# Scores of two differential heads in one run, with the work around the runs in a written order

## The chip, the cores and the metric

The kernel runs on one core of a Trainium2 chip. The metric is the time of one execution on the device in microseconds (us); the time given for a kernel is the median of its runs. The engines are TensorE (PE, matmuls; its weight loads are listed as PEld), VectorE (DVE), ScalarE (ACT), GpSimd (POOL) and SyncE (SP, which issues the loads of weights).

## The reference

A two-layer encoder over 256 tokens of 2048 features, in float32. One layer, with the parts that the change does not touch in a line each:

```python
h = rmsnorm(x, g_mix[i])
dq, dk, dv, cq, ckv, kr, ga, gb = split(h @ w_in[i])
# differential attention: 8 heads, two softmax maps of 64 features each
dq, dk = apply_partial_rope(dq), apply_partial_rope(dk)
scores = einsum('bqhcd,bkhcd->bhcqk', q, k) * 64 ** -0.5
probs = softmax(scores)
weights = probs[:, :, 0] - lam * probs[:, :, 1]
od = einsum('bhqk,bkhe->bqhe', weights, dv)
od = rmsnorm(od, g_subln[i]) * (1 - lam_init)
# latent attention: 8 heads, q and k from low-rank latents, one shared rotary key
om = latent_attention(q_nope, q_rope, k_nope, k_rope, v_mla)
m = sigmoid(ga) * (od @ w_branch_diff[i]) + sigmoid(gb) * (om @ w_branch_mla[i])
x = x + m @ w_out[i]
x = x + swiglu(rmsnorm(x)) ; x = x + sigmoid(rmsnorm(x) @ w_ple_gate[i]) * (p[i] @ w_ple_in[i])
```

## The kernel before, in words

**Precision.** Activations and weights are kept as two parts in TensorE's fast float32 format, a high part and a low part (the rest). A product of a 128-column block of weights with activations is made of pairs of matmuls (`emit`): one of the high weights with both parts of the activations, 512 columns (line 226), and one of the low weights with the high part, 256 columns (line 230). A product over 2048 features has 16 such pairs and one PSUM bank of 512 float32 as its accumulator.

**Weights.** `piece` loads up to eight 128x128 blocks by SP's queue into a buffer `w32` (line 198), ScalarE makes the high part `whi` (line 201) and VectorE the low part `wlo` (a subtraction by the helper at line 78). There are four buffers for loads and three for high parts, so the preparation runs ahead of TensorE by as many pieces.

**Products leave PSUM** in `joined`: ScalarE copies one half (line 256), VectorE adds the other. `split` makes the two parts of a result.

**The differential stage** of a layer goes through these functions. `queries_keys(h)` makes query and key of head h: two products, each joined, rotated with a shuffle (line 577) and three more operations of VectorE, and split. `scores` multiplies them in three terms (high by low, low by high, high by high) for two blocks of 128 queries. The two maps of a head have 64 features each, so their matmuls use 64 rows of the array, one map the upper and one the lower half; they are issued in turns, twelve to a head (line 428). `exps` is the softmax: maximum on VectorE (line 434), exponential and sum on ScalarE (line 437), reciprocal on VectorE (line 438). `diff_weights` joins the two maps (ScalarE line 691, VectorE line 81). `turned` transposes the weights by four matmuls with the identity (line 446) and `diff_out` multiplies them with the values in eight matmuls (line 701). `settle` normalizes four heads and transposes them (line 716).

**Order.** `pipelined` traces the scores of head h+1 ahead of the transposes of head h, and takes steps of the generator `beside` in between: keys of the latent heads (`keys_up`), queries and keys of the next differential head, the shared rotary key (`narrow`, line 414, and `rotated`, line 380), gates and latent queries. What is traced is not yet the order on the engines. A scheduler takes each engine's instructions in the order in which a simulated run has them ready, those traced earlier first; `keep_in_program_order` ties an instruction behind the one traced before it on the same engine, for the order of issue only. After the differential stage come the latent heads (`mla_weights`, `mla_out`, scores also at line 428, in full height), the two branches, the output product, the feed-forward part and the last gate.

**PSUM.** The eight banks are three pools: four banks `mm` for products, two `S` for scores, two `at` for the rest.

Of the kernel before, what the change touches and what calls it, by code (L numbers as in the profile page):

```python
# [56 lines left out]
def encoder(ctx, tc, x, p, positions, cols, lams, wq, wk, wv, wcq, wckv, wkr, wga, wgb,  # L57
# [9 lines left out]
    ps_mm = pool("ps_mm", 4, space=PSUM)  # L67
    ps_s = pool("ps_s", 2, space=PSUM)
# [5 lines left out]
    def bank(ps=ps_at, tag="at", name="at", shape=(P, 2 * T)):  # L74
        return ps.tile(list(shape), F32, tag=tag, name=name)
# [344 lines left out]
    def scores(*maps):  # L420


        Ss = [bank(ps_s, "S", "S", (P, 2, T)) for _ in maps]
        for b in range(2):
            for j in range(len(maps[0])):
                for S, pairs in reversed(list(zip(Ss, maps))):
                    q, k = pairs[j]
                    PE.matmul(S[:, b, :], q[:, b * P : (b + 1) * P], k, start=j == 0, stop=j == len(pairs) - 1)  # L428
        return Ss
# [97 lines left out]
    for L in range(DEPTH):  # L527
# [72 lines left out]
        def keys_up(n):  # L600
            for acc in pair(w_kn[L, n : n + 2], ckv):
                kn.append(operand(fb(len(kn), F32R)))
                split(kn[-1], joined(acc))
# [22 lines left out]
        def beside():  # L626

            for h in range(2, DH):
                if h < 6:
                    keys_up(2 * h - 4)  # L630
                elif h == 7:
                    rotated(joined(narrow(wkr[L], ua)), crm, srm)
                yield
                queries_keys(h)
                yield
            for n in (8, 0, 2, 10):
                if n == 0:
                    settle(0)
                gate(wga, gate_a, next(todo))
                queries_up(n)  # L640
                yield
            settle(4)
            for n in (4, 6):
                gate(wga, gate_a, next(todo))
                queries_up(n)
            gate(wga, gate_a, next(todo))

# [32 lines left out]
        fill = beside()  # L680
# [3 lines left out]
        def diff_weights(h):  # L684
            q, k = qk[h]
            E = [weights(), weights("E1")]
            halves = [slice(c * 64, (c + 1) * 64) for c in range(2)]
            r = [exps(S, e, 0.125) for S, e in zip(scores(*(three(q[d], k[d]) for d in halves)), E)]
            ts(r[1], r[1], neg_lam[:, L : L + 1], None, ALU.mult)
            for b in range(2):  # L690
                A.activation(E[0][:, b, :], E[0][:, b, :], AF.Copy, scale=r[0][:, b : b + 1])
                stt(E[0][:, b, :], E[1][:, b, :], r[1][:, b : b + 1], E[0][:, b, :], ALU.mult, ALU.add)
            return E[0]
# [36 lines left out]
        pipelined(diff_weights, diff_out, DH, lambda: next(fill, None))  # L730
        for _ in fill:
            pass
# [4 lines left out]
        def mla_weights(h):  # L737
            E = weights()
            t = slice(h % 2 * T, (h % 2 + 1) * T)
            S, = scores(three(qn[h], kn[h]) + [(qr[h // 2][:, t], krs[1][:, t]), (qr[h // 2][:, t], krs[0][:, :T])])  # L740
            r = exps(S, E, MLA_SCALE)
            for b in range(2):
                ts(E[:, b, :], E[:, b, :], r[:, b : b + 1], None, ALU.mult)
            return E
# [179 lines left out]
    def S_bank():  # L924
        return operand(bank(ps_s, "S", "S", (P, 2, T)))

    def mm_bank():
        return bank(ps_mm, "mm", "mm")

# [12 lines left out]
    t0 = [transposed(0, q, get()) for q, get in enumerate((S_bank, S_bank, mm_bank, mm_bank))]  # L942
# [13 lines left out]
    t1.append(transposed(1, 3, S_bank()))  # L956
# [92 lines left out]
```

## Time and profile before

| what | value |
|---|---|
| time, median of 3 runs (lowest to highest) | 2825.21 us (2825.15 to 2825.63) |
| the profiled execution | 2825.27 us |
| its span in the trace | 2823.5 us |
| granted clock of TensorE | 0.999 |
| PE busy | 2815.7 us, 16691 matmuls |
| DVE busy | 2080.0 us |
| ACT busy | 1532.0 us |
| matmuls at line 428 of 64 rows | 192 |

A row of the timeline gives the start of an instruction (or of several of one kind) in us, its length, engine, line, operation, output and inputs with their shapes, and the count. Matmuls are pipelined: one starts long before the one ahead has ended, so what a matmul costs TensorE is the time from its start to the next start, and the lengths overlap. A row of the chain gives start, length, engine and line. A row of the groups gives after the bar the busy time in us and the mean of one in ns, and after the second bar the engine's idle time ahead of them. A row of the waits says who waited for whom, for how many us in total, how often, and the longest.

### The profile page before, as it was taken

The numbers are of one execution on the slowest core, as the hardware profiler recorded it, in microseconds if no ns is written. First come the engines' busy times: TensorE is split into PE (matmuls) and PEld (weight loads), VectorE is DVE, ScalarE is ACT, GpSimd is POOL, SyncE is SP. The second block draws the span as 40 slices with busy tenths as digits, with TensorE's granted clock in tenths as the row PEclk, the third lists the DMA queues.
The fourth block names the chain that finished last, engine by engine and source line by source line (L and its number), as shares of the span: only waits on it lengthen the run. The fifth ranks groups of instructions, "written<-read, shape, count | busy, mean of one in ns | idle before, by whom it ended". The sixth has DMA issues, their size and how long they took to land.

```text
span 2823.5 us, 43989 instructions
## 1 busy us (share of the span) xinstructions
PE 2815.7 (100%) x16691; PEld 2489.4 (88%) x16691; DVE 2080.0 (74%) x3566; ACT 1532.0 (54%) x2554; POOL 3.1 (0%) x17
## 2 busy tenths in 40 slices
PE   9999999999999999999999999999999999999999
PEld 8888988888888888888888889888888888888888
DVE  8898668776666666677869976687766666666777
ACT  7676546554444444455646765465544444444556
POOL 0000000000000000000000000000000000000000
PEclk9999999999999999999999999999999999999999
DMA  7545455555665566566554454555556655655654
GB/s 247 174 162 172 157 187 198 194 193 194 186 200 193 188 195 197 193 193 193 194 193 166 157 172 158 194 198 193 194 193 189 199 193 185 202 194 194 193 193 157
DMA packets 158180, 531.36 MB, mean 188 GB/s; under 512 B 17168, under 2 KB 25360, under 8 KB 157968
## 3 DMA queue, kind: packets, MB, share of 16 engines
q1 hardware_dynamic: 157536, 527.96, 56.8%
q8 instruction: 131, 2.15, 0.3%
q10 hardware_dynamic: 432, 0.59, 0.1%
q14 instruction: 81, 0.66, 0.1%
HBM read 526.39 MB, written 2.10 MB: 187 GB/s over the span
## 4 chain that ended last, share of the span: by engine, by line
PE 100%; DMA 0%; DVE 0%; ACT 0%; DVEq 0%; issue 0%
PE mm L226 61%; PE mm L230 31%; PE S L428 1%; PE mmv L501 1%; PE mmv L502 1%; PE mmv L503 1%; PE at L446 1%; PE at L701 1%; PE mm L848 0%; PE at L757 0%; PE mm L414 0%; PE at L716 0%; PE mmv L472 0%; DMA gcol<-in_cols 0%; PE at L339 0%; PE at L307 0%
## 5 line engine op out<-in xcount | busy, mean ns | idle before, releaser
L201 ACT ACTIVATE whi<-w 128x1024 fp32r<-128x1024 f32 (+2 forms) x1038 | 1064.3, 1026 | 1225.6 <-issue 592.8
L78 DVE TENSOR_TENSOR wlo<-w,whi 128x1024 fp32r<-128x1024 f32 (+2 forms) x1038 | 1225.7, 1181 | 645.7 <-ACT whi L201 635.1
L226 PE MATMUL mm<-ub,whi 128*128 128x512 f32 x3936 | 1340.5, 389 | 0.0
L226 PE MATMUL mm<-ua,whi 128*128 128x512 f32 x3712 | 1274.8, 390 | 0.0
L230 PE MATMUL mm<-ub,wlo 128*128 128x256 f32 x3936 | 1084.6, 276 | 0.0
L230 PE MATMUL mm<-ua,wlo 128*128 128x256 f32 x3712 | 1027.8, 277 | 0.0
L226 PEld LDWEIGHTS mm<-ub,whi 128*128 128x128 f32 x3936 | 737.7, 188 | 152.4
L226 PEld LDWEIGHTS mm<-ua,whi 128*128 128x128 f32 x3712 | 696.2, 188 | 141.2
L230 PEld LDWEIGHTS mm<-ub,wlo 128*128 128x128 f32 x3936 | 738.8, 188 | 1.3
L230 PEld LDWEIGHTS mm<-ua,wlo 128*128 128x128 f32 x3712 | 697.0, 188 | 1.9
L78 DVE TENSOR_TENSOR a<-mm,join 128x256 f32<-128x256 f32 (+1 forms) x423 | 174.9, 417 | 1.7 <-ACT join L877 1.4
L256 ACT ACTIVATE join<-mm 128x256 f32<-128x256 f32 x452 | 165.8, 368 | 6.5 <-PE mm L230 5.8
L78 DVE TENSOR_TENSOR xT<-xT,mm 128x256 f32<-128x256 f32 x256 | 106.9, 420 | 41.5 <-PE mm L230 37.6
L78 DVE TENSOR_TENSOR a<-a,row 128x256 f32<-128x256 f32 (+1 forms) x209 | 87.6, 422 | 5.9
L78 DVE TENSOR_TENSOR a<-a 128x256 f32<-128x256 f32 x120 | 50.9, 426 | 4.0
L78 DVE TENSOR_TENSOR ua<-a,ua 128x256 fp32r<-128x256 f32 x120 | 50.0, 418 | 1.0 <-ACT ua L264 1.0
L264 ACT ACTIVATE ua<-a 128x256 fp32r<-128x256 f32 x120 | 48.2, 403 | 2.6 <-DVE a L78 2.6
L437 ACT ACTIVATE E<-S,nm 128x256 f32<-128x256 f32 x96 | 44.2, 472 | 8.1 <-DVE nm L84 8.0
L501 PE MATMUL mmv<-whi,ua 128*128 128x512 f32 x124 | 47.2, 392 | 0.0
L502 PE MATMUL mmv<-whi,ua 128*128 128x512 f32 x124 | 47.0, 392 | 0.0
L503 PE MATMUL mmv<-wlo,ua 128*128 128x512 f32 x124 | 41.2, 391 | 0.0
L78 DVE TENSOR_TENSOR ssq<-ssq,sq 128x256 f32<-128x256 f32 x96 | 40.2, 419 | 0.3 <-ACT sq L294 0.3
(214 smaller groups left out, 1211.6 us busy)
## 6 DMA issues: line engine op xcount, KB each, us to landing
w<-in_w_gate SPq DMA_DIRECT2D x176, 512.0 KB, 4.5
w<-in_w_up SPq DMA_DIRECT2D x176, 512.0 KB, 4.6
w<-in_w_down SPq DMA_DIRECT2D x128, 512.0 KB, 4.2
w<-in_wga SPq DMA_DIRECT2D x64, 512.0 KB, 3.7
w<-in_wgb SPq DMA_DIRECT2D x64, 512.0 KB, 3.7
w<-in_w_out SPq DMA_DIRECT2D x64, 512.0 KB, 3.9
w<-in_w_pg SPq DMA_DIRECT2D x64, 512.0 KB, 4.7
w<-in_w_down SPq DMA_DIRECT2D x64, 384.0 KB, 3.6
```

The costliest lines, as they stand in the source:

```text
L78: return V.tensor_tensor(out=o, in0=a, in1=b, op=op)
L201: last_split[:] = A.activation(hi[:, s], w[:, s], AF.Copy), tt(lo[:, s], w[:, s], hi[:, s].bitcast(F32), ALU.subtract)
L226: lead = PE.matmul(acc, hi[:, s], u, start=start, stop=False)
L230: rest = PE.matmul(acc[:, T:], lo[:, s], u[:, :T], start=False, stop=stop)
L256: A.activation(t, acc[:, T:], AF.Copy)
L264: return A.activation(hi, src, AF.Copy), tt(lo, src, hi.bitcast(F32), ALU.subtract)
L428: PE.matmul(S[:, b, :], q[:, b * P : (b + 1) * P], k, start=j == 0, stop=j == len(pairs) - 1)
L437: last_exp[0] = A.activation(E[:, b, :], S[:, b, :], AF.Exp, bias=nm[:, b : b + 1], scale=scale, accum_out=sm[:, b : b + 1])
L446: PE.transpose(tp[:, kb, b * P : (b + 1) * P], W[:, b, kb * P : (kb + 1) * P], ident)
L501: PE.matmul(banks[k][b], xh, hi[:, s], start=c == 0, stop=False)
L502: PE.matmul(banks[k][b], xl, hi[:, s], start=False, stop=False)
L503: last_mm[:] = [PE.matmul(banks[k][b], xh, lo[:, s], start=False, stop=c == n - 1)]
```

## The change

The scores of two heads are traced in one call, 24 matmuls, each tied behind the one traced before it on TensorE. The pools `mm` (4 banks) and `S` (2) become one pool of six; a run of two heads takes four of them. The generator and `pipelined` give way, in the differential stage, to a written order of four pairs: scores and softmax of both heads, work that stands beside, the transposes of both, work that stands ahead of the outputs, the outputs of both. Keys-up products, which were traced ahead of the next queries and keys, now stand behind them. The latent heads keep `pipelined`; their scores take a bank of the pool of six. At the end of the kernel the banks that were taken from `S` come from that pool too.

```diff
-    ps_mm = pool("ps_mm", 4, space=PSUM)
-    ps_s = pool("ps_s", 2, space=PSUM)
+    ps_mm = pool("ps_mm", 6, space=PSUM)
     ps_at = pool("ps_at", 2, space=PSUM)
...
-    def scores(*maps):
-        Ss = [bank(ps_s, "S", "S", (P, 2, T)) for _ in maps]
-        for b in range(2):
-            for j in range(len(maps[0])):
-                for S, pairs in reversed(list(zip(Ss, maps))):
-                    q, k = pairs[j]
-                    PE.matmul(S[:, b, :], q[:, b * P : (b + 1) * P], k, start=j == 0, stop=j == len(pairs) - 1)
+    def S_bank():
+        return mm_bank().rearrange("p (b t) -> p b t", b=2)
+    def scores(*heads):
+        Ss = [[S_bank() for _ in maps] for maps in heads]
+        for banks, maps in zip(Ss, heads):
+            for b in range(2):
+                for j in range(len(maps[0])):
+                    for S, pairs in reversed(list(zip(banks, maps))):
+                        q, k = pairs[j]
+                        m = PE.matmul(S[:, b, :], q[:, b * P : (b + 1) * P], k, start=j == 0, stop=j == len(pairs) - 1)
+                        if len(heads) > 1:
+                            tc.keep_in_program_order(m)
         return Ss
...
-        def diff_weights(h):
-            q, k = qk[h]
-            E = [weights(), weights("E1")]
+        def diff_weights(h0):
             halves = [slice(c * 64, (c + 1) * 64) for c in range(2)]
-            r = [exps(S, e, 0.125) for S, e in zip(scores(*(three(q[d], k[d]) for d in halves)), E)]
...
+            pairs = [[three(qk[h][0][d], qk[h][1][d]) for d in halves] for h in (h0 + 1, h0)]
+            Ws = []
+            for Ss in scores(*pairs):
+                E = [weights(), weights("E1")]
+                r = [exps(S, e, 0.125) for S, e in zip(Ss, E)]
...
+                Ws.append(E[0])
+            return Ws[::-1]
...
-        pipelined(diff_weights, diff_out, DH, lambda: next(fill, None))
-        for _ in fill:
-            pass
+        def weighed_pair(h, *work):
+            Ws = diff_weights(h)
+            beside, ahead = work[:-1], work[-1]
+            for act, *arg in beside:
+                act(*arg)
+            outs = [diff_out(h + j, Ws[j]) for j in range(2)]
+            for part in outs:
+                next(part)
+            for act, *arg in ahead:
+                act(*arg)
+            for part in outs:
+                next(part, None)
+
+        queries_keys(2)
+        weighed_pair(0, (queries_keys, 3), (keys_up, 0), ((queries_keys, 4),))
+        weighed_pair(2, (queries_keys, 5), (keys_up, 2), ((queries_keys, 6),))
+        weighed_pair(4, (queries_keys, 7), (keys_up, 4), ((settle, 0), (gate_and_queries, 8)))
+        weighed_pair(6, (gate_and_queries, 0), (keys_up, 6), (shared_key,), ((gate_and_queries, 2),))
+        gate_and_queries(10)
+        settle(4)
+        for n in (4, 6):
+            gate_and_queries(n)
+        gate(wga, gate_a, next(todo))
```

In `weighed_pair`, `next(part)` is the transposes of a head and `next(part, None)` its output.

More of the change, by code (lines that the diff above doesn't have):

```diff
@@ L418, in three, with mm_bank @@
         return [(q[:, :T], k[:, T:]), (q[:, T:], k[:, :T]), (q[:, :T], k[:, :T])]
-    def scores(*maps):
-        Ss = [bank(ps_s, "S", "S", (P, 2, T)) for _ in maps]
-        for b in range(2):
-            for j in range(len(maps[0])):
-                for S, pairs in reversed(list(zip(Ss, maps))):
-                    q, k = pairs[j]
-                    PE.matmul(S[:, b, :], q[:, b * P : (b + 1) * P], k, start=j == 0, stop=j == len(pairs) - 1)
+    def mm_bank():
+        return bank(ps_mm, "mm", "mm")
+    def S_bank():
+        return mm_bank().rearrange("p (b t) -> p b t", b=2)
+    def three(q, k):
+        return [(q[:, :T], k[:, T:]), (q[:, T:], k[:, :T]), (q[:, :T], k[:, :T])]
+    def scores(*heads):
[8 more added lines that the diff above has]
+                            tc.keep_in_program_order(m)
         return Ss
@@ L624, in encoder, with shared_key, gate_and_queries @@
         queries_keys(1, lambda: latent_norm(ckv, "g_kv_latent", rkv, lcols[0]), lambda: latent_norm(cq, "g_q_latent", rq, lcols[1]))
[L626 to L645, printed above, removed]
+        def shared_key():
+            rotated(joined(narrow(wkr[L], ua)), crm, srm)
+        def gate_and_queries(n):
             gate(wga, gate_a, next(todo))
+            queries_up(n)
         def gate(w, store, n):
@@ L677, in sigmoid @@
             tc.add_manual_dep(si.ins, last_exp[0].ins.name, NO_SYNC, reason="one change of tables")
-        fill = beside()
         od, ods = [], ub[:8]
         ssd = stat.tile([P, 2 * DH], F32, tag="ssd", name="ssd", bufs=1)
-        def diff_weights(h):
-            q, k = qk[h]
-            E = [weights(), weights("E1")]
+        def diff_weights(h0):
             halves = [slice(c * 64, (c + 1) * 64) for c in range(2)]
-            r = [exps(S, e, 0.125) for S, e in zip(scores(*(three(q[d], k[d]) for d in halves)), E)]
[L689 to L693, printed above, removed]
+            pairs = [[three(qk[h][0][d], qk[h][1][d]) for d in halves] for h in (h0 + 1, h0)]
[3 more added lines that the diff above has]
+                r = [exps(S, e, 0.125) for S, e in zip(Ss, E)]
+                ts(r[1], r[1], neg_lam[:, L : L + 1], None, ALU.mult)
+                for b in range(2):
+                    A.activation(E[0][:, b, :], E[0][:, b, :], AF.Copy, scale=r[0][:, b : b + 1])
+                    stt(E[0][:, b, :], E[1][:, b, :], r[1][:, b : b + 1], E[0][:, b, :], ALU.mult, ALU.add)
+                Ws.append(E[0])
+            return Ws[::-1]
         def diff_out(h, W):
@@ L739, in mla_weights @@
             t = slice(h % 2 * T, (h % 2 + 1) * T)
-            S, = scores(three(qn[h], kn[h]) + [(qr[h // 2][:, t], krs[1][:, t]), (qr[h // 2][:, t], krs[0][:, :T])])
+            (S,), = scores([three(qn[h], kn[h]) + [(qr[h // 2][:, t], krs[1][:, t]), (qr[h // 2][:, t], krs[0][:, :T])]])
             r = exps(S, E, MLA_SCALE)
@@ L922, in store @@
         tc.keep_in_program_order(nc.sync.dma_start(out[b, :, q * 2 * T : (q + 2) * 2 * T], o))
[L924 to L928, printed above, removed]
     def steps(which, n):
@@ L941, in encoder @@
         steps(which, n)
-    t0 = [transposed(0, q, get()) for q, get in enumerate((S_bank, S_bank, mm_bank, mm_bank))]
+    t0 = [transposed(0, q, get()) for q, get in enumerate((mm_bank, mm_bank, mm_bank, mm_bank))]
     t1 = [transposed(1, 0, mm_bank())]
@@ L955, in encoder @@
         store(0, 2 * j, parts_[j])
-    t1.append(transposed(1, 3, S_bank()))
+    t1.append(transposed(1, 3, mm_bank()))
     for j in range(2):
```

## The prediction

> **What bounds the kernel now.** The page's busy times come first.
>
> ```profile
> span 2823.5 us, 43989 instructions
> PE 2815.7 (100%) x16691; PEld 2489.4 (88%) x16691; DVE 2080.0 (74%) x3566; ACT 1532.0 (54%) x2554; POOL 3.1 (0%) x17
> ```
>
> TensorE (PE) is the bound. The list of waits for PE says how much of its time is idle over the whole kernel:
>
> ```profile
> PE at L517 <- DVE ones L123: 1.1, 1, 1.1
> PE mmv L472 <- ACT whi L201: 0.3, 1, 0.3
> ```
>
> That is 1.4 us, both at the start. So no wait can be removed by this change; a gain must come from matmuls that follow each other at less than full pace, and a loss from a wait that is not there today. The profiled execution took 2825.27 us, 1.8 us more than its span, and the median of the three runs is 2825.21, so the sum can be made against 2825.3 and read as the median.
>
> Where is PE slow? A busy PE hides it, so I read starts, not durations, in the timeline of PE. The chain of work names the places: in the first layer the rows of differential scores (L428) are eight runs of twelve, the first and the last of them here, and eight more lie in the second layer.
>
> ```profile
> 106.52 0.89 PE S L428 x12
> ...
> 206.72 0.89 PE S L428 x12
> ```
>
> The last of the eight lies alone among products:
>
> ```profile
> 206.33 0.39 PE L226 MATMUL mm<-ua,whi 128*128 128x512 f32 x1
> 206.65 0.96 PE L428 MATMUL S<-fa,ub 64*128 64x256 f32 x12
> 207.54 0.39 PE L230 MATMUL mm<-ua,wlo 128*128 128x256 f32 x1
> 207.77 0.39 PE L226 MATMUL mm<-ua,whi 128*128 128x512 f32 x1
> 208.00 0.28 PE L230 MATMUL mm<-ua,wlo 128*128 128x256 f32 x1
> 208.11 0.39 PE L226 MATMUL mm<-ua,whi 128*128 128x512 f32 x1
> ```
>
> In undisturbed products an L226 takes 0.23 us to the next start (207.77 to 208.00), an L230 0.11 (208.00 to 208.11), a pair 0.34. Ahead of the run the L226 takes 0.32 (206.33 to 206.65): entry costs 0.09. The run takes 0.89. Behind it the first L230 takes 0.23 (207.54 to 207.77): exit costs 0.12. What would twelve scores take without any edge? They work in pairs, one on each 64-row half of the array, with 256 columns each. The nearest row is the latent heads' full-height scores, also 256 columns:
>
> ```profile
> 283.21 1.16 PE S L428 x10
> ```
>
> That is 0.116 for one, so 6 x 0.116 = 0.70 for six pairs. A run of twelve thus carries 0.19 inside it, 0.09 ahead and up to 0.12 behind.
>
> **The change: fewer runs.** In five of a layer's eight runs the four transposes (L446) of the head before follow at once, as here:
>
> ```profile
> 138.31 0.28 PE L230 MATMUL mm<-ua,wlo 128*128 128x256 f32 x1
> 138.51 0.96 PE L428 MATMUL S<-fa,ub 64*128 64x256 f32 x12
> 139.41 0.66 PE L446 MATMUL at<-ident,E 128*128 128x128 f32 x4
> 139.82 0.47 PE L226 MATMUL mm<-ua,whi 128*128 128x512 f32 x1
> 140.13 0.28 PE L230 MATMUL mm<-ua,wlo 128*128 128x256 f32 x1
> 140.25 0.40 PE L226 MATMUL mm<-ua,whi 128*128 128x512 f32 x1
> ...
> 143.75 0.40 PE L226 MATMUL mm<-ua,whi 128*128 128x512 f32 x1
> ```
>
> Entry is 0.20 - 0.11 = 0.09 again and the run 0.90; the transposes take 0.41 and the first L226 0.31, which is 0.08 over. Transposes away from a run:
>
> ```profile
> 222.91 0.60 PE L446 MATMUL at<-ident,E 128*128 128x128 f32 x4
> 223.27 0.36 PE L230 MATMUL mm<-ub,wlo 128*128 128x256 f32 x1
> 223.47 0.40 PE L226 MATMUL mm<-ub,whi 128*128 128x512 f32 x1
> ```
>
> 0.36, and 0.20 for the L230, 0.09 over. So with transposes behind it the run's exit costs only 0.05. Before, per layer: 8 x (0.09 + 0.89) + 5 x 0.05 + 3 x 0.12 = 8.45 us. After, four runs of 24, each 0.89 + 0.70 = 1.59 (twelve more scores at the inner pace), with products right behind them as written: 4 x (0.09 + 1.59 + 0.12) = 7.20. That saves 1.25 us a layer, **2.5 us** in two.
>
> [...]
>
> **The change: neighbours.** Both heads' outputs (L701) come, as written, right ahead of the next pair's run; three times a layer. No row shows a run behind L701. The bounds are 0 and the whole entry, 0.09; the nearest row, transposes behind a run, saved 0.12 - 0.05 = 0.07. I take that: 6 x 0.07 = **0.4 us**. Merging two outputs, or two sets of transposes, saves nothing:
>
> ```profile
> 143.98 1.05 PE L701 MATMUL at<-vals,wt 128*128 128x128 f32 x8
> 144.79 0.36 PE L230 MATMUL mm<-ua,wlo 128*128 128x256 f32 x1
> 144.99 0.40 PE L226 MATMUL mm<-ua,whi 128*128 128x512 f32 x1
> ```
>
> 0.81 for eight and 0.09 over on the L230 behind: 0.90, eight at 0.11, the pace of four transposes with their 0.09 (0.45). This work has no edge.
>
> **The change: the cadence behind a break.** From 140.25 to 143.75 ten pairs take 3.50 us, 0.350 each and not 0.340. Behind the lone run they take 0.34 at once. By the timeline the products stay at 0.350 where the first matmul behind a run and its transposes is an L226 (a new product, or one resumed at its high part), until the next break, and at 0.340 where it is an L230. Four of a layer's eight runs are of the first kind, with some 61 slow pairs: 0.6 us. After, a pair's run has 36 pairs of matmuls behind it (32 of queries and keys, 4 of keys up) to the transposes. All four slow would be 4 x 36 x 0.01 = 1.4 us a layer, 0.8 more than now; none slow, 0.6 less. In two layers that is +1.7 or -1.2. I see no ground for either end, as the start falls half and half now: half of 1.4 against 0.6 is +0.1 a layer, **+0.2 us**.
>
> **The change: order, waits and banks.** The written order moves keys-up products, the shared key, gates and settling by one or two products, with their weight loads on SP's queue, and past each other. I cost that at nothing while weight preparation stays ahead of PE, as it does now:
>
> ```profile
> ACT whi L201 <- PE mm L226: 16.2, 14, 2.3
> ```
>
> Between 107 and 223 us ScalarE waits 16.2 us for a free weight buffer, that is, for PE. Each score is now pinned behind what was traced before it on PE. If a head's keys were not split yet, or one of the four score banks not free, every product queued behind would stand too, and through the buffers ScalarE and SP's loads. The heads of a pair are made before the products that stand ahead of the run, at least one whole pair of products (32 x 0.34 = 10.9 us) earlier, except at the very first, where queries and keys of head 2 are put in between. Four score banks of six leave two for the products; they need one at a time, plus one being read. Price: nothing, and some tenths of a us per run if wrong. The bank pool elsewhere (latent heads, last transposes) changes names only: PE waits for no bank in the rows above.
>
> Sum: -2.5 - 0.4 + 0.2 = -2.7, so 2825.3 - 2.7 = **2822.6 us**.
>
> **Rivals.** *First: the cadence gives it back.* All runs are followed by a new product's L226, which "long products behind" suggests, and L701 ahead saves nothing: -2.5 + 1.7 = -0.8, so 2824.5. For it: the program order. Against: the scheduler resumes half-done products behind half of today's runs.
>
> *Second: the runs are not made.* The pin holds a score behind its predecessor, but nothing holds a product from coming between them, if the second head's keys or banks come late in the scheduler's reckoning. Then there are sixteen runs as now: 2825.3. Against: none of today's sixteen runs of twelve is broken, and without a pin.
>
> *Third, slower: VectorE.* It is nearly full in this stage.
>
> ```profile
> 107.00:223.00 116.00, 116.00 (x748) 101.65 (x745) 110.52 (x278) 88.17 (x225) 0.00 (x0) 1.00 0.48 160
> ```
>
> The columns are length, PE, PEld, DVE, ACT: VectorE is busy for 110.52 of 116, 95%. Softmax of one head costs it these, of which a head has two, two, two, two and one:
>
> ```profile
> L434 DVE TENSOR_REDUCE nm<-S 128x2 f32<-128x512 f32 x16 | 10.3, 683 | 0.0
> L81 DVE SCALAR_TENSOR_TENSOR E<-E,rsum,E 128x256 f32<-128x256 f32 x16 | 7.1, 479 | 0.1
> L438 DVE RECIPROCAL rsum<-sm 128x2 f32<-128x2 f32 x16 | 2.5, 159 | 0.5 <-ACT E L437 0.3
> L84 DVE TENSOR_SCALAR nm<-nm 128x2 f32<-128x2 f32 x16 | 2.1, 161 | 0.0
> L84 DVE TENSOR_SCALAR rsum<-rsum,neg_lam 128x2 f32<-128x2 f32 x8 | 1.8, 224 | 0.1
> ```
>
> 2 x (0.683 + 0.479 + 0.159 + 0.161) + 0.224 = 3.19 us. Two heads at once put 3.2 us more ahead of the weights' low parts (wlo) of the products behind. The tightest lead of a wlo today, by counting pieces, is here (VectorE, then PE's first use of it):
>
> ```profile
> 112.28 1.22 DVE L78 TENSOR_TENSOR wlo<-w,whi 128x1024 fp32r<-128x1024 f32 x1
> 114.34 0.28 PE L230 MATMUL mm<-ua,wlo 128*128 128x256 f32 x1
> ```
>
> 0.84 us. Most pieces have 3 to 5. The mechanism decides where the lead is under 3.2 us: at 0.84 PE would wait 2.4, in eight pairs 19 us (2841.5); at 2.2 it waits 1.0, and 8.0 - 2.7 makes 2830.6, which I take for this rival. For it: the 95%. Against: the tight spot stands behind the latent norms, and the change puts the first softmax later than that; over a whole pair's 27 us the work is the same; the 12 us behind a run absorb part of it. [...]
>
> **How the numbers follow.** Forecast 0.58, first rival 0.20, second 0.08, third 0.14. The forecast's own range is 2821.2 (no slow cadence) to 2824.0. The range reaches from 2820.5, for costs of runs a little larger than I read, over the first two rivals to 2827.0, with a mild third. About 0.2% (5.6 us) is what a measurement of this kernel can tell from no change. Faster by more would be below 2819.6: removing all edges of all runs, (8.45 - 8 x 0.70) x 2 = 5.7, and all slow cadence, 1.2, would just get there, so 0.03. Slower by more, above 2830.9, is half of the third rival, 0.07. The rest, 0.90, is within.
>
> **What would show it.** In the chain, four runs of 24 a layer of some 1.6 us each. In PE's timeline, entries of 0.09 and exits of 0.12 at these alone. Pairs at 0.34 or 0.35 behind them settle the cadence; it is wrong if a run followed by an L226 goes at 0.34. PE's list of waits must stay at the two rows of the start; a row "PE ... <- DVE wlo L78" would be the third rival, one naming a split or an exponential the order. The forecast is wrong if the sum of these differs from -2.7 by more than the cadence's 1.7.

## The result and the profile after

The changed kernel takes **2846.82 us** (median of 6 runs, 2846.23 to 2850.12) against 2825.36 (6 runs, 2825.10 to 2826.49): 21.5 us slower, ratio 1.0078 [1.0067, 1.0089]. The forecast was 2822.6 us, with a range up to 2827.0 and a chance of 0.07 for a result above 2830.9. This one lies even above the 2841.5 that the prediction worked out for its worst rival. The profiled execution took 2847.97.

The page's span and busy times, after:

```profile
span 2846.2 us, 43933 instructions
PE 2820.5 (99%) x16691; PEld 2496.5 (88%) x16691; DVE 2082.1 (73%) x3566; ACT 1534.1 (54%) x2554; POOL 3.1 (0%) x17
```

The span grew by 22.7 us. TensorE (PE) has the same 16,691 matmuls; its busy time grew by 2820.5 - 2815.7 = 4.8 and its idle time by (2846.2 - 2820.5) - (2823.5 - 2815.7) = 17.9. Two questions follow: what does PE wait for, and why is the same work longer? The list of waits of PE, after (us in total, times, longest), answers the first:

```profile
PE at L699 <- DVE ub L80: 7.5, 2, 3.8
PE mm L437 <- DVE fa L77: 5.9, 2, 3.0
PE mm L225 <- ACT whi L200: 2.0, 2, 1.8
PE mm L229 <- DVE wlo L77: 1.5, 2, 0.8
...
```

Before there were two rows, 1.4 us together, both at the start. These four rows are 16.9 us and come at three places in each layer. I call a place where TensorE stands idle a stand, and these three the first, second and third stand.

**First stand: the first run of scores waits for a key (L437 for fa).** PE's timeline around it:

```profile
116.87 0.28 PE L229 MATMUL mm<-ua,wlo 128*128 128x256 f32 x1
120.11 2.93 PE L437 MATMUL mm<-fa,ub 64*128 64x256 f32 x24 [2.96 <-DVE fa L77]
122.97 0.75 PE L225 MATMUL mm<-ua,whi 128*128 128x512 f32 x1
```

The key is head 1's. Between its product and the run stand the 64 matmuls of head 2, 10.9 us, so that the product ended some 10.9 us ahead of the run's place (117.0), at 106.1. ScalarE copies half of it at 107.17 and makes the key's high part at 118.30:

```profile
118.30 0.41 ACT L263 ACTIVATE fa<-a 128x256 fp32r<-128x256 f32 x1
```

Of VectorE's (DVE's) steps for it these are the first, the last sum and the split (the low part):

```profile
109.45 0.42 DVE L77 TENSOR_TENSOR a<-mm,join 128x256 f32<-128x256 f32 x1
...
116.59 0.42 DVE L77 TENSOR_TENSOR a<-a,sh 128x256 f32<-128x256 f32 x1
...
119.64 0.42 DVE L77 TENSOR_TENSOR fa<-a,fa 128x256 fp32r<-128x256 f32 x1
```

Six operations of some 0.4 us, 2.5 us of work, take from 109.45 to 120.06, since latent norms, four weight parts (wlo) and head 2's query stand between them in the same queue. A part of the way, some 1.3 us, is ScalarE's: the sum is ready at 117.01, and a weight part and a copy go ahead of its high part. From the end of the product to the end of the split are 14.0 us, and 14.0 - 10.9 is the stand. The window ahead of the run shows that VectorE is full (columns: length, PE, PEld, DVE, ACT, POOL, granted clock, share and GB/s of the transfers).

```profile
107.00:117.00 10.00, 10.00 (x60) 8.75 (x58) 9.87 (x22) 5.31 (x10) 0.00 (x0) 1.00 0.55 175
```

It was as full in the same window of the kernel before, and the same key was as late there: its product ended at 106.02 and its split at 120.50, 14.5 us later. But the run that needs it came at 124.07.

```profile
107.00:117.00 10.00, 10.00 (x63) 8.70 (x60) 10.00 (x25) 9.00 (x24) 0.00 (x0) 1.00 0.41 132
120.08 0.42 DVE L78 TENSOR_TENSOR fa<-a,fa 128x256 fp32r<-128x256 f32 x1
```

So the change did not make the key late. It asks for it earlier.

**Second stand: weight parts come late after the first pair's softmax.** Layer 1, PE's timeline:

```profile
1544.07 0.28 PE L229 MATMUL mm<-ua,wlo 128*128 128x256 f32 x1
1546.11 0.51 PE L225 MATMUL mm<-ua,whi 128*128 128x512 f32 x1 [1.77 <-ACT whi L200]
1547.37 0.58 PE L229 MATMUL mm<-ua,wlo 128*128 128x256 f32 x1 [0.75 <-DVE wlo L77]
```

Here ScalarE is the full engine, and not VectorE. The softmax of both heads, with a table load of 1.28 us ahead of it (from 1538.46), goes through it in one piece, and the next high parts of weights stand behind; the low part needs the high part first. The window of the softmax, and the high parts behind it:

```profile
1538.46:1545.00 6.54, 5.88 (x35) 4.94 (x34) 3.25 (x14) 6.53 (x22) 0.00 (x0) 1.00 0.00 0
1545.00 1.58 ACT L200 ACTIVATE whi<-w 128x1024 fp32r<-128x1024 f32 x2
```

ScalarE is busy for 6.53 of 6.54 us and VectorE for 3.25. In layer 0 the two waits are 0.24 and 0.76.

**Third stand: the outputs of heads 4 and 5 stand behind the settling of heads 0 to 3.**

```profile
202.71 0.60 PE L714 MATMUL at<-ident,fa 128*128 128x128 f32 x4
206.94 3.78 PE L699 MATMUL at<-vals,wt 128*128 128x128 f32 x16 [3.63 <-DVE ub L80]
210.65 2.41 PE L437 MATMUL mm<-fa,ub 64*128 64x256 f32 x24
212.99 0.50 PE L225 MATMUL mm<-ua,whi 128*128 128x512 f32 x1
```

The settling's transposes (L714) and the outputs share the two `at` banks. VectorE empties the last of the former only at 206.41, because a weight part, joins and a split are ahead of it in the queue; ScalarE's high parts of the same banks come at 204.37:

```profile
206.41 0.86 DVE L80 SCALAR_TENSOR_TENSOR ub<-at,gsub,ub 128x256 fp32r<-128x256 f32 x2
```

**Why the same matmuls take longer.** The windows of the first run and of the third stand's outputs:

```profile
120.11:122.97 2.86, 2.86 (x24) 2.64 (x25) 2.31 (x8) 0.42 (x1) 0.00 (x0) 0.50 0.55 183
206.94:210.65 3.71, 3.71 (x16) 3.49 (x16) 2.69 (x9) 1.53 (x6) 0.00 (x0) 0.50 0.34 120
```

The granted clock is 0.50 in both. Undisturbed in the same trace, outputs and a run take this:

```profile
148.95 1.95 PE L699 MATMUL at<-vals,wt 128*128 128x128 f32 x16
150.83 1.68 PE L437 MATMUL mm<-fa,ub 64*128 64x256 f32 x24
152.44 0.50 PE L225 MATMUL mm<-ua,whi 128*128 128x512 f32 x1
```

So a run of 24 takes 1.61 (150.83 to 152.44) and not 2.86, sixteen outputs 1.88 and not 3.71. By starts, half clock costs some 1.3 + 0.3 at the first stand of layer 0 (the run, and the L225 behind it), 1.8 + 0.7 at the third (outputs, and 2.34 for the run), 1.6 at the second and 1.5 at the third stand of layer 1 (granted clock 0.50 from 1546.91 to 1550.32 and from 1622.00 to 1625.41): 7.2 us. The busy time grew by 4.8 only, so by this estimate the rest of the work is about 2.4 us shorter than before. That is near the sum of the prediction's terms, but the experiments below do not bear it out where no half clock has to be taken off.

### The profile page after: what moved, and what is told of

Same layout as the page of the kernel before. It is cut to its first block, busy times and chain, and to the rows that moved or that the text cites. A ratio compares the mean times of both kernels' runs of the same rounds, so it can differ in the third digit from the quotient of the medians.

```text
span 2846.2 us, 43933 instructions
## 1 busy us (share of the span) xinstructions
PE 2820.5 (99%) x16691; PEld 2496.5 (88%) x16691; DVE 2082.1 (73%) x3566; ACT 1534.1 (54%) x2554; POOL 3.1 (0%) x17
## 4 chain that ended last, share of the span: by engine, by line
PE 98%; DVE 1%; ACT 1%; DMA 0%; issue 0%; DVEq 0%; SPq 0%; ACTq 0%
PE mm L225 60%; PE mm L229 30%; PE mmv L513 1%; PE mmv L514 1%; PE mmv L512 1%; PE mm L437 1%; PE at L699 1%; PE at L457 0%; DVE wlo L77 0%; PE mm L866 0%; PE at L775 0%; PE mm L413 0%; DVE a L77 0%; ACT whi L200 0%; ACT E L448 0%; DVE nm L445 0%
## 5 line engine op out<-in xcount | busy, mean ns | idle before, releaser
L225 PE MATMUL mm<-ub,whi 128*128 128x512 f32 x3936 | 1339.7, 389 | 0.0
L225 PE MATMUL mm<-ua,whi 128*128 128x512 f32 x3712 | 1275.3, 391 | 2.0 <-ACT whi L200 2.0
L229 PE MATMUL mm<-ub,wlo 128*128 128x256 f32 x3936 | 1084.2, 276 | 0.0
L229 PE MATMUL mm<-ua,wlo 128*128 128x256 f32 x3712 | 1027.0, 277 | 1.5 <-DVE wlo L77 1.5
L225 PEld LDWEIGHTS mm<-ub,whi 128*128 128x128 f32 x3936 | 737.7, 188 | 151.1
L225 PEld LDWEIGHTS mm<-ua,whi 128*128 128x128 f32 x3712 | 697.2, 188 | 145.7 <-ACT whi L200 2.6
L229 PEld LDWEIGHTS mm<-ub,wlo 128*128 128x128 f32 x3936 | 738.9, 188 | 1.6
L229 PEld LDWEIGHTS mm<-ua,wlo 128*128 128x128 f32 x3712 | 697.8, 188 | 3.3 <-DVE wlo L77 2.1
L448 ACT ACTIVATE E<-mm,nm 128x256 f32<-128x256 f32 x96 | 44.4, 472 | 19.0 <-DVE nm L83 19.0
```

What stands on the lines that cost most here:

```text
L225: lead = PE.matmul(acc, hi[:, s], u, start=start, stop=False)
L229: rest = PE.matmul(acc[:, T:], lo[:, s], u[:, :T], start=False, stop=stop)
L448: last_exp[0] = A.activation(E[:, b, :], S[:, b, :], AF.Exp, bias=nm[:, b : b + 1], scale=scale, accum_out=sm[:, b : b + 1])
```

## The experiments

Each time is a median with its range and its ratio to the kernel before on the same chip (2825.3 to 2825.5 there); the expectations give the theories as they stood then. At first I held the stands for two separate misplacements (the first run one product too early, the settling ahead of outputs), against a rival by which VectorE's lateness only shows there and would come up elsewhere.

**The first run later.** Head 3's queries and keys go ahead of the first run too, and the work behind shifts along.

```diff
+        queries_keys(3)
-        weighed_pair(0, (queries_keys, 3), (keys_up, 0), ((queries_keys, 4),))
+        weighed_pair(0, (queries_keys, 4), (keys_up, 0), ((queries_keys, 5),))
...
```

> Only the written order is changed: queries and keys of head 3 are made ahead of the first run too, and all work beside the later runs moves up by one product pair, so 64 more matmuls (10.9 us) lie between head 1's keys and the run that needs them. Theory 1 (the first run stands for a key that VectorE, full with the latent norms, splits 3 us too late, and the idle time lets TensorE's clock fall to half): the wait 'mm L437 <- DVE fa' and the late weight parts behind it are gone, with the half clock near 120 us and 1547 us; some 5.0 us in the first layer and 6.5 in the second, 2846.8 - 11.5 = 2835; the wait at the outputs of heads 4 and 5 stays. Rival (the run waits for four of six banks, or the burst of two softmaxes is what costs): the wait moves with the run, and the time stays at 2844 to 2848.

2844.48 (2844.05 to 2845.68), 1.0068 [1.0053, 1.0083]. The key is no longer waited for, but two waits that were short or absent took its place; from PE's list:

```profile
PE mm L229 <- DVE wlo L77: 3.6, 4, 0.9
PE at L714 <- DVE ub L80: 3.6, 4, 1.5
```

5.9 us of waits for keys and 2.0 for high parts went, 3.6 at the settling and 2.1 more for low parts came: 2.3 us gained in the time, far less than the first theory's figure.

**The settling moved** from ahead of the outputs of heads 4 and 5 to behind the last run.

```diff
-        weighed_pair(4, (queries_keys, 7), (keys_up, 4), ((settle, 0), (gate_and_queries, 8)))
-        weighed_pair(6, (gate_and_queries, 0), ...
+        weighed_pair(4, (queries_keys, 7), (keys_up, 4), ((gate_and_queries, 8),))
+        weighed_pair(6, (settle, 0), (gate_and_queries, 0), ...
```

> Only settle(0), the scaling and transposing of the first four heads, is moved, from ahead of the outputs of heads 4 and 5 to behind the run of heads 6 and 7. Theory 1 (the outputs stand for one of the two 'at' banks, which settle holds until VectorE has taken its low parts): the wait 'at L699 <- DVE ub' of 3.6 and 3.8 us is gone, with the half clock behind it; 6.2 us in the first layer and 5.4 in the second, 2846.8 - 11.6 = 2835; the first run's wait stays at 3.0 us. Rival (VectorE is simply behind there, whatever stands first): another wait of some 3 us at the same outputs or at the next run, and 2844 to 2848.

2838.84 (2837.19 to 2839.28), 1.0046 [1.0029, 1.0063]: 8.0 us of the 21.5, where 11.6 were expected. The third stand is gone, the first two stay, and waits for high parts are 2.1 us longer than in the changed kernel:

```profile
PE mm L437 <- DVE fa L77: 5.9, 2, 3.0
PE mm L225 <- ACT whi L200: 4.1, 4, 1.6
```

**Both moves at once**, with the shared key in pair 4.

> Both changes of order together; the shared key stands beside heads 4 and 5 and the last latent queries' halves ahead of their outputs, so that settle(0) can stand behind the last run. Theory 1 (the two stands of each layer are the whole loss, and four runs of 24 scores a layer are worth what the forecast worked out): PE waits for nothing but the 1.4 us of the start, granted clock 0.999, and 2825.4 - 2.7 = 2822.7, with 2821.2 to 2824.5 for the pace of the products behind a run. Rival (the burst of two heads' softmax costs in every pair): waits for late weight parts remain, a us or more in each pair, and the time stays above 2829.

2836.48 (2836.15 to 2837.60), 1.0040 [1.0025, 1.0055]. Behind the start no wait is over 1.0 us, and still it is 11 us slower than before; small waits for weight parts and for copied transposes (`wt`) have come in the stands' place:

```profile
PE mm L229 <- DVE wlo L77: 3.0, 4, 0.9
PE at L457 <- ACT wt L462: 1.9, 2, 1.0
...
```

That is the rival's outcome in time and in kind, though in no pair does a weight part cost a whole us. The separate misplacements were not the cause by themselves; the stands are where lateness shows.

**Three `at` banks, five for the rest.**

```diff
-    ps_mm = pool("ps_mm", 6, space=PSUM)
-    ps_at = pool("ps_at", 2, space=PSUM)
+    ps_mm = pool("ps_mm", 5, space=PSUM)
+    ps_at = pool("ps_at", 3, space=PSUM)
```

> The changed kernel with five banks in the common pool and three 'at' banks, order of tracing untouched. Theory 1 (the outputs of heads 4 and 5 stand for an 'at' bank that settle holds): with a third bank the wait 'at L699 <- DVE ub' is gone or under 1 us, and with it some 11 us: 2836; five banks cost the runs nothing. Rival (it is not the bank but VectorE's lateness): the wait stays over 3 us under another releaser, 2844 to 2848. Third possibility: five banks leave a run of four too few, and PE waits for a bank at the runs; then more than 2848.

2843.55 (2843.08 to 2844.17), 1.0064 [1.0049, 1.0079]. This is 3.3 us less than the changed kernel and not the 11 of the first theory. The outputs wait no more, so the stand at them needs that there are only two `at` banks. But the last run of each layer now waits for its key as well; the row of the first stand doubles its count:

```profile
PE mm L437 <- DVE fa L77: 9.9, 4, 3.0
```

**The scores not tied** to their written order on PE (the `keep_in_program_order` of the runs left out).

> The changed kernel without the tie of each score to the matmul traced before it. On TensorE the order stays nearly the same (the last run of a layer moves ahead of the outputs of heads 4 and 5, the first stays 79 matmuls into the second and third head's products). Theory 2 (VectorE, 93% busy in this stage before, is what TensorE waits for, and the written order asks for its results where it is furthest behind): the first run still waits 3 us for its key, 2840 to 2848. Rival (the tie itself holds the queue, and without it products would fill the wait): no wait of over 1 us at line 437, and under 2830.

2843.41 (2842.92 to 2844.89), 1.0064 [1.0049, 1.0079]. The first run stands at the same place and waits as long (longest 3.0). The tie is not the cause of the first stand. What changes is the third stand of layer 0: the last run goes ahead of the outputs there and waits 2.4 us for its own key.

**The common pool alone.** The kernel before, with its order and its runs of twelve, but products and scores from one pool of six banks.

```diff
-    ps_mm = pool("ps_mm", 4, space=PSUM)
-    ps_s = pool("ps_s", 2, space=PSUM)
+    ps_mm = pool("ps_mm", 6, space=PSUM)
...
-        Ss = [bank(ps_s, "S", "S", (P, 2, T)) for _ in maps]
+        Ss = [bank(ps_mm, "mm", "mm").rearrange("p (b t) -> p b t", b=2) for _ in maps]
```

> The kernel before with the common pool of six banks alone, so that scores, twelve at a time, may take more than two banks. Forecast's reading: banks cost nothing, PE waits for nothing, 2825.4 with at most 1.5 either way, since runs fall elsewhere among the products. Rival (with more banks the scheduler brings runs and softmax closer together, and VectorE falls behind as in the changed kernel): PE waits for late keys or weight parts, 2830 or more.

2909.48 (2908.49 to 2909.92), 1.0296 [1.0279, 1.0313]: 84 us slower, where the expectation by the forecast's reading was no change. All of the waits behind the start lie in the two differential stages. PE's list:

```profile
PE mm L427 <- DVE fa L77: 21.5, 8, 4.4
PE at L445 <- DVE E L80: 18.1, 2, 9.1
```

The first head's transposes now stand 8 product matmuls behind its run, where they wait 9.1 us for the softmax, and the second run right behind them; before, 95 product matmuls lay between the two runs.

```profile
118.48 1.21 PE L445 MATMUL at<-ident,E 128*128 128x128 f32 x4 [9.05 <-DVE E L80]
119.62 1.65 PE L427 MATMUL mm<-fa,ub 64*128 64x256 f32 x12
```

So the division of the banks sets the order as much as any line of the program. I read it thus: two score banks had kept each run back until the softmax before it had read its banks. The written order of the change takes most of this harm away again.

**Less work for VectorE.** Three kernels leave out the rotation of the differential queries and keys (shuffle, product with the sines, sum): 128 VectorE operations fewer. First the kernel before and the changed kernel so:

```diff
-                sh = scratch("sh", 2)
-                V.stream_shuffle(sh, a, ROPE16)
-                tt(sh, sh, sr, ALU.mult)
                 tt(a, a, cr, ALU.mult)
-                tt(a, a, sh, ALU.add)
```

> The kernel before with part of the computation left out: queries and keys of the differential heads are not rotated (a shuffle, a product and a sum on VectorE less for each of 16 products a layer, some 1.0 us each, 16 us a layer). A control for the next run. TensorE has no wait to lose, so all theories expect 2825.4 within 1.5; only where the runs fall among the products may change.

> The changed kernel with the same part left out (no rotation of the differential queries and keys), so that VectorE has 16 us a layer less to do in the same written order. Theory 2 (VectorE's lateness is the cause of the waits at the first run, of the late weight parts behind it and of the wait at the outputs): the first run's wait of 3.0 us is gone, and the others shrink to under 1 us each; 2823 to 2829. Theory 1 (the order alone, above all the 'at' banks that settle holds, is the cause of the wait at the outputs): that wait stays at 3 us or more in each layer with the half clock behind it, 2834 or more.

Before: 2826.80 (2826.28 to 2828.06), 1.0005 [0.9996, 1.0015], no gain. Changed: 2834.77 (2833.73 to 2836.30), 1.0033 [1.0020, 1.0046], 12.1 us faster than with the rotation. Each theory had half of it. The first stand is gone, of the second 0.6 us is left, and the third stays:

```profile
PE at L695 <- DVE ub L80: 6.6, 2, 3.3
```

and VectorE has room ahead of the first run, 8.14 of 10 us and not 9.87:

```profile
107.00:117.00 10.00, 10.00 (x62) 8.67 (x62) 8.14 (x14) 5.50 (x11) 0.00 (x0) 1.00 0.53 164
```

Leaving the rotation out is worth nothing before and 12 us after. Not all of this is VectorE's load, since three of the key's own six steps, 1.3 us, go too; but the first stand was 3.0, so its queue counts for the rest. The second stand shrinks with the first: ScalarE makes a high part 5.2 us behind the start of the run, ahead of its exponentials, where in the changed kernel none comes until 10.7 us behind it.

**The settling moved and the rotation left out.**

> The changed kernel with settle(0) behind the last run and with the rotation of the differential queries and keys left out, so that neither the 'at' banks nor VectorE should make TensorE wait. Theory 2 (VectorE's lateness at the first run and settle ahead of the outputs are the whole loss; runs of 24 are worth what was read from the rows): PE waits for nothing behind the start. The trace of the changed kernel prices a run of 24 behind outputs at 0.10 + 0.25 + 0.11 us over the even pace, against twice 0.36 before: 0.26 less a pair, 2.1 in eight; the 36 pairs behind each run at 0.350 instead of 0.340 cost 0.35, 2.8 in eight, against 1.2 before. So 2825.5 - 2.1 + 1.6 = 2825.0, 2824 to 2827. Rival (two softmaxes in a row cost by themselves, through ScalarE's exponentials ahead of the weights): waits of over 0.5 us behind each run, 2829 or more.

2827.82 (2827.64 to 2828.49), 1.0009 [1.0000, 1.0018]. No wait over 0.9 us is left behind the start, and it takes 1.0 us more than the kernel before without rotation, and 0.8 more than the top of what was expected (2824 to 2827). PE still waits 2.6 us for weight parts (L225 1.7, L229 0.9), which that kernel does not; without these the change would be some 1.6 us ahead by this estimate, and a part of it would not be its own, since in that kernel one run in each layer is broken in two. PE's busy time is that of the kernel before with the rotation, 2815.7 us, at a mean granted clock of 0.999:

```profile
PE 2815.7 (100%) x16691; PEld 2489.1 (88%) x16691; DVE 2048.9 (73%) x3438; ACT 1530.9 (54%) x2554; POOL 3.1 (0%) x17
```

Its first run is the cleanest row for the prediction's own terms:

```profile
117.00 0.28 PE L229 MATMUL mm<-ua,wlo 128*128 128x256 f32 x1
117.21 1.65 PE L437 MATMUL mm<-fa,ub 64*128 64x256 f32 x24
118.78 0.50 PE L225 MATMUL mm<-ua,whi 128*128 128x512 f32 x1
119.12 0.28 PE L229 MATMUL mm<-ua,wlo 128*128 128x256 f32 x1
```

Entry 0.21 - 0.11 = 0.10, the run 1.57, exit 0.34 - 0.23 = 0.11.

**The cadence.** To that kernel, the product behind a run (and each gate) begins with two high parts and two low parts in a row.

```diff
-            lead = PE.matmul(acc, hi[:, s], u, start=start, stop=False)
+            if not (twice and j == 1):
+                lead = PE.matmul(acc, hi[:, s], u, start=start, stop=False)
+            if twice and j == 0:
+                PE.matmul(acc, hi[:, (at + 1) * P : (at + 2) * P], us[1], start=False, stop=False)
```

> As the run before it in this call (no rotation, settle(0) behind the last run), but the first product behind each run begins with its first two high parts one behind the other and then the two low parts, as a test of the pace. Theory (pairs stay at 0.350 us behind a run only as long as high and low parts strictly alternate; two high parts in a row end it): the pairs behind a run go at 0.340 and the time falls by 8 x 0.35 = 2.8 us against that run, to about 2822.5. Rival (the pace is set by the run itself, or by which buffer holds the weights): the pairs stay at 0.350, and the time is the same within 0.5.

2829.82 (2829.30 to 2830.42), 1.0016 [1.0007, 1.0025], 2.0 us slower. The pace behind the run does go to 0.34 at once:

```profile
119.43 0.39 PE L226 MATMUL mm<-ua,whi 128*128 128x512 f32 x1
...
119.77 0.39 PE L226 MATMUL mm<-ua,whi 128*128 128x512 f32 x1
```

But 2.8 us were not there to be gained: by matmul starts, only four of the eight runs of the kernel without it have the slow pace behind them, 1.4 us in all. And the gates of the next stage, outside these runs, became slower with the doubled start (by some 1.2 us a layer, from matmul starts).

**The written order alone**, with the banks of before (four and two), a run for each head, not tied.

> The written order alone: the pools of before (four banks for products, two for scores) and a run of twelve for each head, not tied, in the changed kernel's order of tracing. Theory 2 (what hurts is when VectorE is asked, so the order by itself loses, whatever the pools): waits for late keys, weight parts or at the outputs of heads 4 and 5, 2832 to 2846. Rival (the common pool of six is what lets runs come too close; with two score banks the order is harmless): PE waits under 2 us behind the start, 2824 to 2828.

2836.18 (2835.70 to 2836.63), 1.0038 [1.0023, 1.0053]. PE waits 2.5 us in all, and its mean clock is 1.000. The loss is in broken runs: with one of two score banks free, six scores of one map go alone. A whole run of twelve and a half one:

```profile
124.44 0.97 PE L438 MATMUL S<-fa,ub 64*128 64x256 f32 x12
...
131.35 0.98 PE L438 MATMUL S<-fa,ub 64*128 64x256 f32 x6
```

Six of one map alone take as long as twelve in pairs. There are 24 runs in place of 16, and eight more at 0.9 us and some 0.2 of entry and exit are 8.9 us (an estimate) of the 10.9 lost. So neither theory had it right: the time falls into the range of the one, but not by waits; PE hardly waits, as the other said, but the time is lost. What this run shows besides: with two score banks and no merged runs the same written order has none of the three stands. They come from the order and the common pool together.

**GpSimd takes a step over.** The settling moved, nothing left out, and the product with the sines on GpSimd.

```diff
-                tt(sh, sh, sr, ALU.mult)
+                nc.gpsimd.tensor_tensor(out=sh, in0=sh, in1=sr, op=ALU.mult)
```

> Nothing left out: the changed kernel with settle(0) behind the last run, and one of the products of the rotation (the shuffled half by the sine) computed on GpSimd instead of VectorE, which gives VectorE 16 x 0.33 = 5 us a layer back. Theory 2 (VectorE is what TensorE waits for): the waits at the first run and for weight parts shrink by half or more, from 2838.8 to about 2830 (2826 to 2834). Rival (GpSimd is slow, and the keys come later by what it takes longer): the first run waits longer than 3 us, above 2839.

2834.30 (2833.87 to 2834.61), 1.0031 [1.0020, 1.0043]: 4.5 us less than the moved settling by itself, just above the range expected (2826 to 2834). The first stand halves, with all steps of the key kept. The clock does not fall (1.000 in the mean), and still PE is busy for 1.0 us more than before; the rest of the 9.0 us is waits.

```profile
PE mm L437 <- DVE fa L77: 2.7, 2, 1.4
PE 2816.7 (99%) x16691; PEld 2491.7 (88%) x16691; DVE 2081.3 (73%) x3534; ACT 1531.7 (54%) x2554; POOL 35.3 (1%) x49
```

**Banks divided again.** By then one question was open: the first run comes behind 79 product matmuls in a row, and PE does nothing else while it waits (2.96 us). I thought that score banks taken ahead leave none for products. So two banks for products, four for scores (the values' second half and the end's transposes moved to score banks).

```diff
-    ps_mm = pool("ps_mm", 6, space=PSUM)
+    ps_mm = pool("ps_mm", 2, space=PSUM)
+    ps_s = pool("ps_s", 4, space=PSUM)
...
-        return mm_bank().rearrange("p (b t) -> p b t", b=2)
+        return bank(ps_s, "S", "S").rearrange("p (b t) -> p b t", b=2)
```

> The changed kernel with its merged runs and written order as they are, but the six common banks divided again: two for products, four for scores (the values' second half and the end's transposes take score banks, so that nothing else has to wait). In the built order the first run then stands behind 118 product matmuls instead of 79. Bank theory (the run is issued before VectorE has made its key because score banks taken ahead of time leave the products none, so that they can't be put in front): the 3.0 us stand at the first run and the half clock behind it go, and so does the late weight behind it; the stand of the settled outputs (3.6 to 3.8 us for ub) stays or shrinks: 2838 to 2843 us. Rival (VectorE alone is late, and the banks only name places): a run of 24 waits for a key or a weight by 2.5 us or more in the first stage again, in another place: 2845 to 2850 us. Second rival: two banks are too few for the products, PE waits many times by tenths: over 2850 us.

2930.96 (2924.95 to 2934.96), 1.0378 [1.0361, 1.0395]. The run now comes behind 118 product matmuls and waits for no key; so the banks do decide its place. But the stand has only moved: behind the run a product waits 6.1 us for VectorE to empty a product bank (ScalarE, with its softmax, is the fuller of the two there, 5.94 us of 6.25 and VectorE 4.66), and the same wait comes all over the kernel, in stages with no differential scores too.

```profile
PE mm L226 <- DVE a L78: 32.2, 18, 6.1
PE mm L226 <- DVE xT L78: 14.5, 20, 1.9
```

The second rival of that expectation held: two product banks are too few. What divided banks would do with enough of them for the products is not shown: every kernel here shares out eight.

**The same with the settling moved, and with GpSimd besides.**

> As the run with divided banks, and the settling of heads 0 to 3 moved from ahead of the outputs of heads 4 and 5 to behind the last run. Bank theory: no stand of 3 us is left and the clock stays full; what remains over the kernel before is the score runs' place and VectorE's share: 2828 to 2834 us (the same move alone took 8 us off the changed kernel). Rival (VectorE alone is late): as with the move alone, 2836 to 2840 us, with one stand of 3 us for a key.

> As the run with divided banks and moved settling, and the product of the shuffled copy with the sines goes to GpSimd (VectorE loses about 0.4 us for each rotation). If VectorE's fullness still costs time there, 3 to 5 us less than without it (2825 to 2831 us); if the divided banks already keep PE ahead of VectorE, within 1.5 us of it, since no PE wait for VectorE is left to shorten.

2929.56 (2925.92 to 2933.80), 1.0369 [1.0353, 1.0384], and 2936.18 (2930.69 to 2944.13), 1.0394 [1.0372, 1.0416]. The product banks bound both, so neither edit can show what it is worth; they say nothing more on VectorE.

No version here beats the kernel before.

## Why the prediction was wrong

**Fewer runs, -2.5: right in its rows, not shown in the total.** A run of 24 takes 1.57 to 1.61 (1.59 forecast), entry 0.10 and exit 0.11 alone among products. In the changed kernel PE's busy time less the price of half clock fell by about that. But in the two kernels with moved settling in which the clock did not fall (0.999 and 1.000), PE is busy for 2815.7 and 2816.7 us, and not for less than the 2815.7 of before. By matmul starts the runs of the second of them take 1.6 us less in all than before, the outputs 1.2 more and the products 0.7 more. What of this the new order costs by itself stays open.

**Neighbours, -0.4: wrong, small.** Behind outputs a run has its whole entry: sixteen outputs of 0.11 are 1.76, from 148.95 to 150.83 it is 1.88, 0.12 over. The bound of 0 was the right end, and the nearest row, transposes behind a run, was the wrong one to take.

**The cadence, +0.2: about right, by luck.** Behind undisturbed runs it came both ways, at 0.35 to the next break (as at 152.44 and 180.41) and at 0.34 (as behind the run at 1594.37, where 29 pairs take 9.86 us from 1597.15). All eight runs are followed by a high part (L225), so by the prediction's reading all would have been slow. The reading is wrong, as the prediction itself said it would be if a run followed by such a matmul went at 0.34; why they went both ways is not explained.

**Order, waits and banks, 0: the step that failed**, in three sentences of it.
- The heads of a pair are made "at least one whole pair of products (32 x 0.34 = 10.9 us) earlier". They are, and at the very first run, which the sentence sets apart, by no more than that. But 10.9 us is TensorE's time. I did not price the way from a finished product to a split key on a VectorE that is 95% full: 14.0 us at this place. The row that would have said so was in the trace of before: the same key's split there ends 14.5 us behind its product. The price given if this was wrong, "some tenths of a us per run", was too small by a factor of about ten.
- Banks at nothing: "Four score banks of six leave two for the products; they need one at a time, plus one being read." The pool alone costs 84 us without the new order. Two banks for products, held to that number, brought the changed kernel from 2847 to 2931. (That the pool "changes names only" in the latent heads and at the end is not contradicted: PE has no new wait there.)
- Settling was named among the steps that move "by one or two products". I did not ask which banks the outputs behind it need. They need the two that it fills, and its emptying waits in VectorE's queue: two stands of 3.6 to 3.8, and 8.0 us with their half clock, by the settling moved.

**The third rival, VectorE full: the engine right for the dear stands, for which it was not put forward.** I let the softmax burst on VectorE delay the weights' low parts, 8 us. The burst does delay weights, at the second stand, but on ScalarE, whose exponentials and copies stand ahead of the high parts (2.0 us, and 1.5 for low parts behind them). The dearer stands came from keys and settled outputs in VectorE's full queue. I had read the tight leads for one consumer only, the weights. PE did wait for VectorE to empty banks, at the settling (7.5 us) and with divided banks (32.2).

**No wait today was read as slack.** PE waited for nothing before, and VectorE was idle for 5% of the stage: I took that as work that fits. Without rotation the kernel before is no faster and the changed one is by 12 us. The order of before kept PE off VectorE's results until they were there; that its two score banks are what set this order is shown by the common pool alone and by the written order with the banks of before, which has no stand.

**Half clock was not in the sum at all**: about 7 of the 21.5 us.

What stays open: why the common pool puts the first run at the 79th product and divided pools at the 118th is read from the built order, not tested bank by bank; and of the remaining 9.0 us of the kernel with moved settling and GpSimd, 8.0 are waits for keys and weight parts, and no version here with whole runs of 24 and nothing left out is free of waits.

## What to carry to other kernels

Where an engine is 95% full beside the bound one, as VectorE is here (110.52 of 116 us before), the distance from a product to its consumer is to be counted in that engine's queue (14.0 us at the first stand) and not in the bound engine's work (10.9): look for the longest delay from a matmul to its last split in the stage, and keep every new wait farther behind than that. The engine to look at is the one that is full at that very place, VectorE at the key (9.87 of 10 us) and ScalarE behind a softmax of two heads (6.53 of 6.54). A pool of PSUM banks is part of the schedule (the common pool alone cost 84 us): two banks that hold a stage back may be what keeps TensorE from standing. And a stand of 3 to 4 us is to be priced with up to 2.5 us of half clock behind it, as the third stand of layer 0 had (3.63 us, and the granted clock 0.50 behind it).

## What the runs showed of the hardware

- Stands of 2.96 us were followed by 3.41 us at a granted clock of 0.50 in layer 0 (120.14 to 123.55; run of 24: 2.86 us) and by full clock in layer 1 (1.00 from 1534.29 to 1538.00), with the same wait and the same work behind:

```profile
1534.29 1.68 PE L437 MATMUL mm<-fa,ub 64*128 64x256 f32 x24 [2.96 <-DVE fa L77]
1535.89 0.50 PE L225 MATMUL mm<-ua,whi 128*128 128x512 f32 x1
```

  Two waits of 1.77 and 0.75 with a single matmul between them (1544.07 to 1547.37) went with half clock too, 0.50 from 1546.91, within the second wait, to 1550.32. At the third stands it was 0.50 from 205.47 to 212.30 (6.83 us, from before the outputs start at 206.94) and from 1622.00 to 1625.41. Why one stand of 2.96 us had half clock behind it and the other had not is not shown.
- Six half-height scores of one map alone take the time of twelve in pairs (0.91 us each by starts, 131.35 to 132.26 and 124.44 to 125.35, in the run of the written order alone): a run broken so loses the whole of the pairing.
